# Sums of weights and of left factors on VectorE, and weighted values of two heads by turns, in a four-layer float32 transformer kernel on one core

## The chip, the core and the metric

One NeuronCore of a Trainium2 chip runs the whole program. The time is the device time of one execution in microseconds (us). The profiled execution is a single one, taken by the hardware profiler. Engines: TensorE (PE; its weight loads are PEld), VectorE (DVE), ScalarE (ACT), GpSimd (POOL), SyncE (SP, which issues most DMAs).

## What is computed

Two models run one after the other on 512 tokens of width 1024: two layers of the first block, then two layers of the second. Everything is float32. The parts that matter here, cut from the reference:

```python
# first block, per layer: one of two attentions has no positions (4 heads of 64)
z = einsum(q_blk, kt) * scale
log_stay = where(causal, log_sigmoid(-z), 0)
attn = where(causal, exp(log_sigmoid(z) + cumsum_of_later(log_stay)), 0)
o_b = einsum(attn, vt)                       # the weighted values
...
# second block, end of each layer: gated feed-forward, hidden width 2816
up = rmsnorm(x) @ w_gate_up
x = x + (silu(up[..., :2816]) * up[..., 2816:]) @ w_down
```

## The kernel before

Activations are kept transposed (features on the 128 partitions, 512 tokens along a tile) in `self.x`. A float32 product is made of three float32r products: each operand is split into a rounded part and a rest, by an ACT copy (`hi`, `xh`, ...) and a DVE subtraction (`lo`, `xl`, ...); `mm3` (L225 to L227) issues the three matmuls.

The whole program is written out in one order, and each engine executes its own instructions in that order. Weights come through a list of chunks made by `make_plan`. A chunk has raw tiles of 128x1024 (512 KB, loaded by SP, 6 buffers) and units, each a pair `hi`/`lo` made by `put` (L132 on ACT, L133 on DVE; 4 buffers each). `tick` and `product` call `pump`, which emits the units of the chunks to come, and then `step`, which advances every background generator by one piece.

**Feed-forward of the second block.** Hidden tiles 0 to 5 are plain products (`fa`, `fv`). Tiles 6 to 21 go in 16 pairs over both layers (8 a layer, in groups of 3, 2 and 3 and then 3, 3 and 2, with the down projection `fd` of a group behind it). A pair takes seven half-size products (a Strassen-like scheme) in place of eight. For that the weight blocks are added up (`schunks`: `pre` makes two sums before the pair's first unit, `post1` and `post5` one each behind the first and the fifth; `add`, L327, four sums of 128x1024 a pair), and the normalized activations, the left factors, are added up once a layer (`factors`, L1005 to L1013, a background generator that runs while the plain products go on; its `put` splits them at L992 to L996). `spair` runs a pair: seven `product` calls with the keys 11, 1, 2, 4, 12, 3 and 22, of 24 matmuls of 256 columns each (L1049), and between them

- L1083, L1087, L1092: ACT copies `s1`, `p5` and `d` out of PSUM;
- L1094, L1100: DVE forms the gate half by half from the bank `A`; product 3 adds into the same bank, so it waits for L1094;
- L1071: Silu on ACT; L1103: the first half times `s1`, on POOL; L1109: the second half out of PSUM, on DVE; L237 and L238: the split of the result.

Product 11 of the next pair is issued ahead of product 22 of a pair.

**Attention without positions.** `mixer_b` is a background generator beside the projections of the first block. It runs four heads a layer, one after another; heads 2 and 3 follow 0 and 1. For each it ends with the weights `at` (L840, exp on ACT; L844, mask on POOL) and, a step later, four products of float32 with 64 columns of values (L850) into the head's 64 partitions of `po`. In the profile each shows as two instructions. The other attention's three value tiles `va` are made at the start of `mixer1` (L664, ones set by POOL at L666).

For comparison: the attention of the second block's last layer issues its weighted values at L1774 for two heads by turns, with the same shapes as L850.

Of the kernel before, what the change touches and what calls it, by code (L numbers as in the profile page):

```python
# [4 lines left out]
F32 = mybir.dt.float32  # L5
F32R = mybir.dt.float32r
I32 = mybir.dt.int32
AF = mybir.ActivationFunctionType
ALU = mybir.AluOpType
AX = mybir.AxisListType  # L10
MUL, ADD, SUB, MAX = ALU.mult, ALU.add, ALU.subtract, ALU.max
P = 128
S = 512
# [304 lines left out]
def schunks(name, w, c1, c2):  # L318


    b = [block(w, r, 4, c, 256) for r, c in ((0, c1), (0, c2), (512, c2), (512, c1))]

    b11, b12, b22, b21 = b
    box = {}

    def add(c, to, x, y):
        c.nc.gpsimd.tensor_tensor(to, x, y, op=ADD)  # L327

    def pre(c, r):

        box["t"] = c.pf.tile([P, 1024], F32, tag="t0", bufs=1, name=c.nm("t0")).rearrange("p (k c) -> p k c", k=4)
        add(c, box["t"], r[0], r[1])
        add(c, r[1], r[1], r[2])

    def post1(c, r):

        add(c, r[0], r[0], r[1])

    def post5(c, r):

        add(c, r[0], r[0], r[1])

    def temp(c, hi, lo, raws):
        c.put(hi, lo, box.pop("t"))

    u = [dict(unit(4, 256, whole, (b11,), 0), pre=pre, praws=(b11, b12, b22), post=post1),
         unit(4, 256, temp, (b11,), 0),
         unit(4, 256, whole, (b11,), 0),
         unit(4, 256, whole, (b22,), 1),
         dict(unit(4, 256, whole, (b21, b11), 1, 1), post=post5, praws=(b21, b11)),  # L350
         unit(4, 256, whole, (b12,), 1),
         unit(4, 256, whole, (b21,), 1)]
    out = [chunk(name, [], [x]) for x in u]
    out[0]["raws"] = b
    return out
# [116 lines left out]
class Kern(Ctx):  # L472
# [188 lines left out]
    def mixer1(self, l):  # L661
        nc = self.nc

        va = [self.pv.tile([P, 4, 2, 3, 64], F32, tag="va", bufs=3, name=self.nm("va")) for _ in range(3)]  # L664
        for g in range(3):
            nc.gpsimd.memset(va[g][:, :, :, 1], 1.0)  # L666
        vb = self.pv.tile([P, 4, 256], F32, tag="vb", bufs=1, name=self.nm("vb"))
        qT, kT = {}, {}

# [50 lines left out]
        oB = []  # L720
# [9 lines left out]
            self.finish(g)  # L730
        gE = self.bg(self.mixer_a_exp(st))
        v_chunk("v1", va[1], True)
        v_chunk("v2", va[2], True)
        self.finish(gB)
        oA = [None] * 2
        gA = self.bg(self.mixer_a(va, st, oA))
        ga, gb = [], []
# [40 lines left out]
    def mixer_b(self, qT, kT, vb, oB):  # L778
        nc = self.nc
        seg = {0: (0, 0, 512), 1: (1, 0, 384), 3: (1, 384, 128), 2: (2, 0, 256)}  # L780
        nc.scalar.preload_act_table_set("natural_log_exp_and_others")
        for hp in range(2):
            po = None
            for hh in range(2):
                h = 2 * hp + hh
                rs = slice(64 * hh, 64 * hh + 64)
                q, k = qT[("b", hp)], kT[("b", hp)]
                z = [self.ps() for _ in range(3)]
# [37 lines left out]
                for kt in (0, 1, 3, 2):  # L826
# [8 lines left out]
                        continue  # L835
                    for v in (ach, acl):
                        nc.tensor.matmul(z[b][:, o + P:o + n], lhsT=self.nones_r, rhs=v[kt], start=False, stop=(v is acl), skip_group_check=True)
                at = [self.t("at") for _ in range(3)]
                for b in range(3):
                    nc.scalar.activation(at[b][:, 0:wid[b]], z[b][:, 0:wid[b]], AF.Exp)  # L840
                ag = {kt: at[b][:, o:o + n] for kt, (b, o, n) in seg.items()}
# [2 lines left out]
                    nc.gpsimd.affine_select(out=d, in_=d, pattern=[[1, P]], compare_op=ALU.is_gt, fill=0.0, base=0, channel_multiplier=-1)  # L844
                del z, sp, sg, acc, a1, a2, sph, spl, ach, acl
                yield
                if po is None:
                    po = self.ps()
                for kt in range(4):
                    nc.tensor.matmul(po[rs, kt * P:S], lhsT=vb[:, kt, h * 64:(h + 1) * 64], rhs=ag[kt], start=(kt == 0), stop=(kt == 3))  # L850
                if hh == 1:
                    oB.append(self.split(po, "oB"))

    def mixer_a_scores(self, g, qT, kT, st):
        nc = self.nc
# [123 lines left out]
    def factors(self):  # L979
# [2 lines left out]
        nc = self.nc  # L982
        A = self.A = {k: [] for k in ("11", "12", "22", "1", "2", "3", "4")}
        H = (slice(0, 256), slice(256, 512))
        tt = nc.gpsimd.tensor_tensor

        def put(src, keys, scale=None, tiles=None, at=0):
            n = src.shape[-1]
# [12 lines left out]
        for j in range(5):  # L1001
            cur = None
            if j < 4:
                xa, xb = self.t("xa"), self.t("xb")
                for t, k in ((xa, j), (xb, j + 4)):  # L1005
                    nc.scalar.activation(t, self.x[k], AF.Copy, scale=self.ngain(k))
                    tt(t, t, self.Rb, op=MUL)
                a11, a21, a12, a22 = xa[:, H[0]], xa[:, H[1]], xb[:, H[0]], xb[:, H[1]]
                s14, s23 = self.t("s14"), self.t("s23")
                tt(s14[:, H[0]], a22, a21, op=SUB)  # L1010
                tt(s23[:, H[0]], a11, s14[:, H[0]], op=ADD)
                tt(s23[:, H[1]], a21, a11, op=SUB)
                tt(s14[:, H[1]], s23[:, H[0]], a12, op=SUB)  # L1013
                cur = a11, xb, s14, s23
            if last:
                a11, xb, s14, s23 = last
                if j % 2:
                    two = self.ft("Ah"), self.ft("Al")
                put(a11, ("11",), tiles=two, at=256 * ((j - 1) % 2))
                put(s14, ("1", "4"))  # L1020
                put(s23, ("2", "3"), scale=-1.0)
                rest.append(xb)
            last = cur
            yield
# [28 lines left out]
    def ffn(self, l, after, conv):  # L1053
# [22 lines left out]
        def spair(f, ah, al):  # L1076
# [22 lines left out]
            for nt in range(2):  # L1099
                nc.vector.scalar_tensor_tensor(a[nt][:, H[1]], half(A, nt), -1.0, half(p5, nt), op0=MUL, op1=SUB)  # L1100
            g = [act_a(a[nt], f + nt, False) for nt in range(2)]
            for nt in range(2):
                nc.gpsimd.tensor_tensor(g[nt][:, H[0]], g[nt][:, H[0]], half(s1, nt), op=MUL)  # L1103
            yield
            self.product(A, "22", False)

            def out():
# [997 lines left out]
```

## Time and profile before

| | us |
|---|---|
| three runs | 2769.3, 2763.86, 2762.52 |
| median | 2763.86 |
| profiled execution | 2763.89 |
| its span, first to last instruction | 2761.8 |
| PE busy | 2704.5 |
| DVE busy | 1615.7 |
| ACT busy | 1108.2 |
| POOL busy | 554.0 |

The span is what the trace covers; the execution's own time is 2.1 us longer. PE is busy for nearly all of it, so that a change shows in the time where PE idles, runs at a lower clock, or has less to do. "Busy" of PE counts the time in which a matmul is under way.

### The profile page before, as it was taken

The numbers are of one execution on the slowest core, as the hardware profiler recorded it, in microseconds if no ns is written. First come the engines' busy times: TensorE is split into PE (matmuls) and PEld (weight loads), VectorE is DVE, ScalarE is ACT, GpSimd is POOL, SyncE is SP. The second block draws the span as 40 slices with busy tenths as digits, with TensorE's granted clock in tenths as the row PEclk, the third lists the DMA queues.
The fourth block names the chain that finished last, engine by engine and source line by source line (L and its number), as shares of the span: only waits on it lengthen the run. The fifth ranks groups of instructions, "written<-read, shape, count | busy, mean of one in ns | idle before, by whom it ended". The sixth has DMA issues, their size and how long they took to land.

```text
span 2761.8 us, 36222 instructions
## 1 busy us (share of the span) xinstructions
PE 2704.5 (98%) x14462; PEld 2303.4 (83%) x14462; DVE 1615.7 (58%) x2254; ACT 1108.2 (40%) x1672; POOL 554.0 (20%) x509
## 2 busy tenths in 40 slices
PE   8999999999999999999999999999999999999997
PEld 7788888888878888788878887898988888879897
DVE  5644654455455365554566667676756656667655
ACT  4353332333344334332343354343443536534334
POOL 2110210001111011110031105344411001334423
PEclk9999999999999999999999999999999999999999
DMA  5232323332323223322223332232232113223231
GB/s 189 62 93 76 92 92 93 105 99 88 114 67 82 72 92 107 103 95 93 92 92 111 96 103 81 93 122 92 89 90 86 54 47 107 85 84 114 78 107 54
DMA packets 236424, 254.77 MB, mean 92 GB/s; under 512 B 19904, under 2 KB 212672, under 8 KB 235616
## 3 DMA queue, kind: packets, MB, share of 16 engines
q1 hardware_dynamic: 233808, 245.70, 28.9%
q0 software_dynamic: 1440, 5.97, 0.6%
q8 instruction: 113, 1.85, 0.3%
q10 hardware_dynamic: 1008, 0.80, 0.1%
q14 instruction: 55, 0.45, 0.1%
HBM read 248.20 MB, written 2.10 MB: 91 GB/s over the span
## 4 chain that ended last, share of the span: by engine, by line
PE 87%; DVE 5%; ACT 3%; issue 3%; POOL 2%; DMA 0%; ACTq 0%; POOLq 0%; SPq 0%; DVEq 0%
PE ps L225 23%; PE ps L227 23%; PE ps L226 23%; PE ps L1049 11%; DVE lo L133 2%; PE ps L948 1%; ACT hi L132 1%; PE ps L850 1%; PE ps L1722 1%; PE ps L793 1%; PE ps L874 1%; DVE x L656 0%; PE ps L1448 0%; PE ps L963 0%; DVE xl L241 0%
## 5 line engine op out<-in xcount | busy, mean ns | idle before, releaser
L133 DVE TENSOR_TENSOR lo<-raw,hi 128x1024 fp32r<-128x1024 f32 (+2 forms) x515 | 655.0, 1300 | 272.3 <-ACT hi L132 269.7
L225 PE MATMUL ps<-xh,hi 128*128 128x512 f32 x1712 | 676.0, 395 | 11.5 <-ACT hi L132 11.5
L227 PE MATMUL ps<-xh,lo 128*128 128x512 f32 x1712 | 670.2, 391 | 6.5 <-DVE lo L133 6.4
L226 PE MATMUL ps<-xl,hi 128*128 128x512 f32 x1712 | 669.4, 391 | 0.0
L132 ACT ACTIVATE hi<-raw 128x1024 fp32r<-128x1024 f32 (+2 forms) x515 | 505.8, 1012 | 303.7 <-PE ps L226 232.5
L225 PEld LDWEIGHTS ps<-xh,hi 128*128 128x128 f32 x1712 | 323.3, 189 | 80.6 <-ACT hi L132 12.3
L227 PEld LDWEIGHTS ps<-xh,lo 128*128 128x128 f32 x1712 | 323.1, 189 | 77.6 <-DVE lo L133 9.7
L226 PEld LDWEIGHTS ps<-xl,hi 128*128 128x128 f32 x1712 | 323.4, 189 | 65.5 <-issue 0.2
L225 PE MATMUL ps<-acth,hi 128*128 128x512 f32 (+1 forms) x736 | 280.1, 381 | 1.0 <-ACT acth L237 1.0
L226 PE MATMUL ps<-actl,hi 128*128 128x512 f32 (+1 forms) x736 | 279.9, 380 | 0.6 <-DVE actl L238 0.6
L227 PE MATMUL ps<-acth,lo 128*128 128x512 f32 (+1 forms) x736 | 279.6, 380 | 0.0
L1049 PE MATMUL ps<-Ah,hi 128*128 128x256 f32 x896 | 255.0, 285 | 11.0 <-DVE a L1094 9.9
L1049 PE MATMUL ps<-Al,hi 128*128 128x256 f32 x896 | 254.2, 284 | 0.0
L1049 PE MATMUL ps<-Ah,lo 128*128 128x256 f32 x896 | 254.1, 284 | 0.0
L656 DVE TENSOR_TENSOR x<-ps,x 128x512 f32<-128x512 f32 x168 | 115.4, 687 | 176.0 <-PE ps L227 176.0
L1049 PEld LDWEIGHTS ps<-Ah,hi 128*128 128x128 f32 x896 | 172.4, 192 | 13.4 <-ACT hi L132 10.8
L537 POOL TENSOR_TENSOR sq<-sq,sq 128x512 f32<-128x512 f32 (+1 forms) x73 | 97.2, 1337 | 423.7 <-ACT sq L531 423.2
L1073 POOL TENSOR_TENSOR y<-y,Rb 128x512 f32<-128x512 f32 x44 | 57.0, 1295 | 590.5 <-ACT y L1068 590.5
L327 POOL TENSOR_TENSOR raw<-raw,raw 128x1024 f32<-128x1024 f32 x48 | 127.7, 2661 | 234.8 <-DVE lo L133 151.1
L1049 PEld LDWEIGHTS ps<-Al,hi 128*128 128x128 f32 x896 | 172.4, 192 | 0.4
L1049 PEld LDWEIGHTS ps<-Ah,lo 128*128 128x128 f32 x896 | 172.4, 192 | 0.0
L225 PEld LDWEIGHTS ps<-acth,hi 128*128 128x128 f32 x736 | 138.4, 188 | 27.5 <-ACT acth L237 1.4
(401 smaller groups left out, 4082.5 us busy)
## 6 DMA issues: line engine op xcount, KB each, us to landing
raw<-in_w_up SPq DMA_DIRECT2D x88, 512.0 KB, 3.7
raw<-in_ffn_w_gate_up SPq DMA_DIRECT2D x88, 512.0 KB, 3.6
raw<-in_w_in SPq DMA_DIRECT2D x78, 512.0 KB, 4.7
raw<-in_w_down SPq DMA_DIRECT2D x44, 512.0 KB, 4.1
raw<-in_ffn_w_down SPq DMA_DIRECT2D x44, 512.0 KB, 3.8
raw<-in_od_w_in SPq DMA_DIRECT2D x20, 512.0 KB, 3.9
raw<-in_w_o SPq DMA_DIRECT2D x16, 512.0 KB, 3.7
raw<-in_xattn_wkv SPq DMA_DIRECT2D x16, 512.0 KB, 4.5
```

The source lines that it names most:

```text
L132: self.nc.scalar.activation(hi, raw, AF.Copy)
L133: self.nc.vector.tensor_tensor(lo, raw, hi.bitcast(F32), op=SUB)
L225: mm(out, lhsT=wh, rhs=xh, start=first, stop=False)
L226: mm(out, lhsT=wh, rhs=xl, start=False, stop=False)
L227: mm(out, lhsT=wl, rhs=xh, start=False, stop=last)
L327: c.nc.gpsimd.tensor_tensor(to, x, y, op=ADD)
L537: (nc.vector if dve else nc.gpsimd).tensor_tensor(acc[to], acc[to], q, op=ADD)
L656: self.nc.vector.tensor_tensor(self.x[j], ps, self.x[j], op=ADD)
L793: nc.tensor.matmul(z[b][:, o:o + n], lhsT=k[rs, kt * P:(kt + 1) * P], rhs=q[rs, kt * P:S], start=(kt != 3), stop=False, skip_group_check=True)
L850: nc.tensor.matmul(po[rs, kt * P:S], lhsT=vb[:, kt, h * 64:(h + 1) * 64], rhs=ag[kt], start=(kt == 0), stop=(kt == 3))
L1049: mm(o, lhsT=w, rhs=x, start=(first and nt == 0 and j == 0 and i == 0), stop=(j == 3 and i == 2), skip_group_check=True)
L1073: nc.gpsimd.tensor_tensor(t, t, self.Rb, op=MUL)
```

## The change

Four sums of weights a pair (L327), the sums of the left factors (L1010 to L1013) and the product L1103 go from POOL to DVE. The left factors' two scalings (ACT at L1006, POOL at L1007) become one DVE instruction. `factors` gets one more `yield`, between the sums and their split; `spair` has its second `yield` ahead of the product at L1103, not behind it. In `mixer_b` the weights of the first head of a pair are kept in a `va` buffer until those of the second are there; then the eight products of both go by turns. The third `va` tile is made later for that, behind the end of `mixer_b`. Three parts of the diff that only rename are left out.

```diff
     def add(c, to, x, y):
-        c.nc.gpsimd.tensor_tensor(to, x, y, op=ADD)
+        c.nc.vector.tensor_tensor(to, x, y, op=ADD)
...
-        va = [self.pv.tile([P, 4, 2, 3, 64], F32, tag="va", bufs=3, name=self.nm("va")) for _ in range(3)]
-        for g in range(3):
-            nc.gpsimd.memset(va[g][:, :, :, 1], 1.0)
+        va = []
+
+        def new_va():
+            va.append(self.pv.tile([P, 4, 2, 3, 64], F32, tag="va", bufs=3, name=self.nm("va")))
+            nc.gpsimd.memset(va[-1][:, :, :, 1], 1.0)
+        for g in range(2):
+            new_va()
...
         v_chunk("v1", va[1], True)
+        self.finish(gB)
+        new_va()
         v_chunk("v2", va[2], True)
-        self.finish(gB)
...
-                at = [self.t("at") for _ in range(3)]
+                if hh == 0:
+
+                    room = self.pv.tile([P, 4, 2, 3, 64], F32, tag="va", bufs=3, name=self.nm("at")).rearrange("p t a b c -> p (t a b c)")
+                    at = [room[:, S * b:S * b + S] for b in range(3)]
+                else:
+                    at = [self.t("at") for _ in range(3)]
...
-                if po is None:
-                    po = self.ps()
+                if hh == 0:
+                    first = ag
+                    continue
+
+                po = self.ps()
                 for kt in range(4):
-                    nc.tensor.matmul(po[rs, kt * P:S], lhsT=vb[:, kt, h * 64:(h + 1) * 64], rhs=ag[kt], start=(kt == 0), stop=(kt == 3))
-                if hh == 1:
-                    oB.append(self.split(po, "oB"))
+                    for i, a in enumerate((first, ag)):
+                        c = (2 * hp + i) * 64
+                        nc.tensor.matmul(po[64 * i:64 * i + 64, kt * P:S], lhsT=vb[:, kt, c:c + 64], rhs=a[kt], start=(kt == 0), stop=(kt == 3))
+                oB.append(self.split(po, "oB"))
...
-        tt = nc.gpsimd.tensor_tensor
+        tt = nc.vector.tensor_tensor
...
                 for t, k in ((xa, j), (xb, j + 4)):
-                    nc.scalar.activation(t, self.x[k], AF.Copy, scale=self.ngain(k))
-                    tt(t, t, self.Rb, op=MUL)
+                    nc.vector.scalar_tensor_tensor(t, self.x[k], self.ngain(k), self.Rb, op0=MUL, op1=MUL)
...
                 cur = a11, xb, s14, s23
+                yield
...
             g = [act_a(a[nt], f + nt, False) for nt in range(2)]
+            yield
             for nt in range(2):
-                nc.gpsimd.tensor_tensor(g[nt][:, H[0]], g[nt][:, H[0]], half(s1, nt), op=MUL)
-            yield
+                nc.vector.tensor_tensor(g[nt][:, H[0]], g[nt][:, H[0]], half(s1, nt), op=MUL)
```

The order on DVE in the second pair of a group, from the first pair's L1109 (the gate's second half, out of PSUM) to the second pair's L1094. Before:

```order
L1109 TENSOR_TENSOR a_13775<-ps_13673,a_13775 128x256
L238 TENSOR_TENSOR actl_13971<-a_13774,acth_13970 128x512
L238 TENSOR_TENSOR actl_13975<-a_13775,acth_13974 128x512
L133 TENSOR_TENSOR lo_14005<-raw_13563,hi_14004 128x1024
L133 TENSOR_TENSOR lo_14040<-raw_13772,hi_14039 128x1024
L1094 SCALAR_TENSOR_TENSOR a_14013<-ps_13874,d_14044 128x256
```

The same place in the change (L1121 and L1106 there are L1109 and L1094 here, L1116 is the product L1103):

```order
L1116 TENSOR_TENSOR a_13759<-a_13759,s_13690 128x256
L133 TENSOR_TENSOR lo_13914<-raw_13688,hi_13913 128x1024
L133 TENSOR_TENSOR lo_13946<-raw_13721,hi_13945 128x1024
L327 TENSOR_TENSOR raw_13721<-raw_13721,raw_13501 128x1024
L1121 TENSOR_TENSOR a_13759<-ps_13657,a_13759 128x256
L238 TENSOR_TENSOR actl_13959<-a_13759,acth_13958 128x512
L133 TENSOR_TENSOR lo_13989<-raw_13543,hi_13988 128x1024
L327 TENSOR_TENSOR t_13992<-raw_13756,raw_13821 128x1024
L327 TENSOR_TENSOR raw_13821<-raw_13821,raw_13917 128x1024
L133 TENSOR_TENSOR lo_14024<-raw_13756,hi_14023 128x1024
L327 TENSOR_TENSOR raw_13756<-raw_13756,raw_13821 128x1024
L1106 SCALAR_TENSOR_TENSOR a_13997<-ps_13856,d_14028 128x256
```

One sum now stands ahead of the gate's second half, and three more ahead of L1094 of the pair behind it. Of two equal instructions in a row one is shown.

The order on ACT among the plain products, at one step of the left factors (`Ah` is the rounded part of a factor, `hi` of a weight). Before:

```order
L237 ACTIVATE acth_13079<-a_12993 128x512
L1006 ACTIVATE xa_13084<-x_70,prm 128x512
L1006 ACTIVATE xb_13085<-x_74,prm 128x512
L992 ACTIVATE Ah_13096<-xa_13041 128x256
L992 ACTIVATE Ah_13100<-s_13047 128x512
L995 ACTIVATE Ah_13104<-s_13048 128x512
L132 ACTIVATE hi_13133<-raw_12766 128x1024
```

And in the change:

```order
L1083 ACTIVATE a_13343<-a_13343 128x512
L1004 ACTIVATE Ah_13347<-xa_13214 128x256
L1004 ACTIVATE Ah_13351<-s_13218 128x512
L1007 ACTIVATE Ah_13355<-s_13219 128x512
L132 ACTIVATE hi_13384<-raw_13107 128x1024
```

The two scalings are gone from ACT, and the split of a step's sums comes one step later than the sums.

The order on PE where a pair of heads in the first layer ends, in the change; before, the first head's four products stood by themselves some 140 rows earlier:

```order
L863 MATMUL ps_990<-at_671,vb_210 64x512
L863 MATMUL ps_990<-at_929,vb_210 64x512
L863 MATMUL ps_990<-at_671,vb_210 64x384
L863 MATMUL ps_990<-at_930,vb_210 64x384
L863 MATMUL ps_990<-at_671,vb_210 64x256
```

Products of head 0 (`at_671`) and head 1 (`at_929`, `at_930`) now follow each other in turn, into the two halves of one PSUM bank.

## Rows read from the trace of the kernel before

**Rows 1.** The page, part 1: busy time, share of the span and instructions of each engine.

```profile
PE 2704.5 (98%) x14462; PEld 2303.4 (83%) x14462; DVE 1615.7 (58%) x2254; ACT 1108.2 (40%) x1672; POOL 554.0 (20%) x509
```

**Rows 2.** Waits of PE: us in total, times, longest.

```profile
PE ps L225 <- ACT hi L132: 13.4, 4, 7.3
PE ps L1049 <- DVE a L1094: 9.9, 5, 2.0
```

**Rows 3.** Windows: length, busy us (count) of PE, PEld, DVE, ACT, POOL, granted clock, DMA.

```profile
1700.00:1715.00 15.00, 15.00 (x68) 12.42 (x67) 11.46 (x11) 7.33 (x13) 14.69 (x12) 1.00 0.19 57
...
1720.00:1735.00 15.00, 9.69 (x34) 7.03 (x33) 11.91 (x13) 7.53 (x14) 12.00 (x11) 0.77 0.22 71
2420.00:2435.00 15.00, 10.42 (x36) 7.86 (x36) 12.07 (x13) 7.08 (x12) 12.88 (x11) 0.77 0.19 58
```

**Rows 4.** Windows of 10 us around the five waits for L1094; the sum is over five.

```profile
2520.00:2530.00 10.00, 8.02 (x55) 7.84 (x54) 8.59 (x9) 2.70 (x5) 3.54 (x4) 0.83 0.32 107
2615.00:2625.00 10.00, 8.02 (x67) 7.84 (x67) 10.00 (x9) 2.60 (x3) 4.82 (x2) 1.00 0.22 61
sum 50.00, PE 40.09 PEld 39.10 DVE 48.17 ACT 13.43 POOL 23.84; mean PE 8.02 PEld 7.82 DVE 9.63 ACT 2.69 POOL 4.77
```

**Rows 5.** Groups by line on PE, then PE's timeline: start, us, instruction.

```profile
L850 PE MATMUL ps<-at,vb 128*64 128x512 f32 (+3 forms) x64 | 18.9, 439 | 0.0
L1774 PE MATMUL ps<-PT,mv 128*64 128x512 f32 (+3 forms) x64 | 9.5, 439 | 0.0
...
2161.01 2.37 PE L1774 MATMUL ps<-PT,mv 128*64 128x512 f32 x16
```

**Rows 6.** Timeline of DVE in the first group's second pair.

```profile
1803.16 0.74 DVE L1100 SCALAR_TENSOR_TENSOR a<-ps,p 128x256 f32<-128x256 f32 x2
1805.74 3.70 DVE L133 TENSOR_TENSOR lo<-raw,hi 128x1024 fp32r<-128x1024 f32 x3 [1.84 <-ACT hi L132]
1810.52 4.82 DVE L238 TENSOR_TENSOR actl<-a,acth 128x512 fp32r<-128x512 f32 x2 [0.43 <-ACT acth L237]
1815.27 4.56 DVE L133 TENSOR_TENSOR lo<-raw,hi 128x1024 fp32r<-128x1024 f32 x2
1819.76 0.74 DVE L1094 SCALAR_TENSOR_TENSOR a<-ps,d 128x256 f32<-128x256 f32 x2
...
1825.09 0.74 DVE L1100 SCALAR_TENSOR_TENSOR a<-ps,p 128x256 f32<-128x256 f32 x2
```

**Rows 7.** Timeline of POOL in the same pair.

```profile
1811.94 2.85 POOL L327 TENSOR_TENSOR t<-raw,raw 128x1024 f32<-128x1024 f32 x1
1814.87 2.74 POOL L327 TENSOR_TENSOR raw<-raw,raw 128x1024 f32<-128x1024 f32 x1
```

**Rows 8.** DVE while POOL is idle (timeline), and its shortest instructions (by tile: min/median/max).

```profile
1835.42 2.35 DVE L133 TENSOR_TENSOR lo<-raw,hi 128x1024 fp32r<-128x1024 f32 x2
...
1931.08 1.29 DVE L238 TENSOR_TENSOR actl<-a,acth 128x512 fp32r<-128x512 f32 x2 [0.42 <-ACT acth L237]
...
L993 DVE TENSOR_TENSOR Al<-xa,Ah x8: 412/668/1344, 1703.8 to 2433.8; 128x256 fp32r<-128x256 f32 x8
...
L996 DVE SCALAR_TENSOR_TENSOR Al<-s,Ah x8: 678/1766/1800, 1707.1 to 2434.7; 128x512 fp32r<-128x512 f32 x8
```

**Rows 9.** The first stretch of left factors: timelines of PE, ACT and DVE.

```profile
1724.37 0.67 PE L225 MATMUL ps<-xh,hi 128*128 128x512 f32 x1 [2.67 <-ACT hi L132]
...
1723.28 1.99 ACT L132 ACTIVATE hi<-raw 128x1024 fp32r<-128x1024 f32 x2
...
1724.07 1.77 DVE L996 SCALAR_TENSOR_TENSOR Al<-s,Ah 128x512 fp32r<-128x512 f32 x1
1725.76 3.95 DVE L133 TENSOR_TENSOR lo<-raw,hi 128x1024 fp32r<-128x1024 f32 x2
```

**Rows 10.** Groups by line on POOL: busy us, mean ns, idle time before and what ended it.

```profile
L327 POOL TENSOR_TENSOR raw<-raw,raw 128x1024 f32<-128x1024 f32 x48 | 127.7, 2661 | 234.8 <-DVE lo L133 151.1 <-issue 68.2 <-DMA raw<-in_ffn_w_gate_up 14.3
L327 POOL TENSOR_TENSOR t<-raw,raw 128x1024 f32<-128x1024 f32 x16 | 47.2, 2952 | 19.3 <-DMA raw<-in_ffn_w_gate_up 19.3
```

More of the change, by code (lines that the diff above doesn't have):

```diff
@@ L782, in mixer_b @@
         for hp in range(2):
-            po = None
             for hh in range(2):
-                h = 2 * hp + hh
                 rs = slice(64 * hh, 64 * hh + 64)
```

## The prediction

> **What bounds the kernel now.** I read the page first: PE is busy for 2704.5 of 2761.8 us [rows 1], so there is no other engine to relieve as such. A gain can come from three things only: PE's own work, its 57 us of idling, and stretches at a lower granted clock. Then the waits of PE, to see whose they are. Two lines carry 23 us of the idling, and both lie in the second block's feed-forward: PE waits for the rounded weights of ACT (13.4 us, four times), and for L1094 of DVE (9.9 us, five times) [rows 2]. Third, windows around these waits, to see what they cost with the clock in it; fourth, the timelines of DVE, POOL and ACT there, to see what is late. What idles elsewhere (the starts of layers, the end) the change does not touch.
>
> *The stretches of the left factors.* A stretch of 15 us at full rate holds 68 matmuls of 512 columns, 0.221 us each; the two stretches where the left factors are made hold 34 and 36, and their granted clock is 0.77 on average: after PE has idled, a part of them runs at the lower of its two levels, 1.2 and not 2.4 GHz [rows 3]. So 66 matmuls are lost, 14.6 us, of which the two stretches' idling is 5.3 and 4.6 us; the rest is clock. What is late there is not PE's data as such. POOL is busy 14.69 of 15 us [rows 3], while a step of the factors comes with every 24 matmuls, 5.3 us. ACT waits in order for POOL's sums before it can round the next weights, at 1723.28, when PE has stood still for them since 1721.7; and DVE, beside POOL, takes 1.77 us for an instruction whose shortest is 0.68, and 3.95 us for two subtractions that take 2.35 when POOL is idle [rows 8, 9].
>
> *The pairs.* In each of the five places PE stands still for 2.0 us ahead of product 3: PE is busy 40.09 of 50 us, one place also has a clock of 0.83 and 55 matmuls where the next has 67, 12 of 0.12 us or 1.4 us more [rows 4]. That makes 11.3 us. DVE comes to L1094 late: beside POOL's sums of weights (2.85 and 2.74 us) two subtractions take 4.56 us and two splits 4.82 [rows 6, 7]; with POOL idle the same take 2.35 and 1.29 [rows 8].
>
> **The change, part by part.**
>
> *Weighted values by turns.* The same count and the same shapes stand twice in the trace: one head after another, 64 instructions keep PE busy 18.9 us; two heads by turns, 64 take 9.5, since 16 lie in 2.37 us [rows 5]. PE is saturated in the projections that this runs beside, so the 9.4 us come off the end: **-9.4**. From below it could be nothing, if the two heads did not overlap; L1774 has the same halves of a bank, and nothing else to tell it apart, so I take all. The first head's weights wait a few steps in a `va` buffer; nobody else wants that buffer before the last value tile, and behind the late memset on POOL stand only value copies of that tile, which come several steps later. Nothing.
>
> *Left factors on DVE.* Per step POOL loses two scalings and four sums, ACT loses two scalings. DVE gets two instructions of 128x512 at 0.68 and four of 128x256 at 0.41, the shortest of such rows [rows 8]: 3.0 us a step, 12 us a layer. The other end for these is what DVE takes beside POOL, 1.77 [rows 9], but POOL has then little left there (one product with the norm, for each hidden tile). With the split (0.41 and twice 0.68, 1.8 us), a chunk of 48 matmuls (10.6 us) asks of DVE: 3.0 + 1.8, two subtractions 2.35, and two to four instructions of about 0.68, some 9 to 10 us. That is tight but fits, and the extra `yield` puts sums and split into different steps. For the weights that PE now lacks at 1721.7: PE is done with the chunk before the last at 1711.1, two times 5.3 us earlier. DVE is then about 1 us behind with a step of sums; an evacuation 0.7, a piece of the rotation tables 0.6, the split 1.8 with some 0.8 of waiting for ACT, and the two subtractions 2.35 end at about 1718.4, 3.3 us ahead of PE. Carried on in the same way the next two chunks are ready some 1.6 and 2 us ahead. So I take back 13.6 of the 14.6 us and leave 1 us for a late one: **-13.6**. From below: one of the stretches stays as it is, -7.3.
>
> *Sums of weights and the product L1103 on DVE.* Four sums at 1.2 us (half of 2.35, the row with the same shape and inputs) and two products at 0.41 [rows 8] come into DVE's order, 5.6 us a pair, and POOL has nothing left to do there. The other end for a sum is POOL's own mean, 2.66 to 2.95 us [rows 10]. What decides is the way from L1100 of one pair to L1094 of the next, since PE cannot start product 3 before it. Before, it is 1820.50 - 1803.16 = 17.3 us [rows 6]. In the new order: L1100 0.74, the wait for ACT 1.84, three subtractions 3.70, two products 0.8, a sum 1.2, L1109 0.74, the wait 0.43, two splits 1.29, two subtractions 2.35, three sums 3.6, L1094 0.74: 17.4 us. So this way gets no shorter. But it starts earlier. PE's seven products take 1825.09 - 1803.16 - 2.0 = 19.95 us, 2.85 each; product 3 could start 17.1 us behind the end of the last product 3. Before, L1100 itself came nearly 2 us behind that end, because DVE had two more slowed subtractions ahead of it; now these take 1.2 each and L1100 waits only for PE. So PE's stand shrinks from 2.0 us to 0.3, or to 1 where ACT has its copies to make in between; I take 0.7. Five times 1.3, and the 1.4 of clock: **-7.9**. With sums at 2.66 us each place would stand 5.8 us longer, +29 in all; with no stand at all it would be -11.3.
>
> New waits: `pre` on DVE waits for raw weights. POOL's sums waited 33.6 us for DMAs in all [rows 10], but early, when POOL had nothing to do; DVE comes to `pre` only behind L238 or the first `x` of the down projection, some 8 us later, when they have landed. Behind it would stand L1094 or the sums into `x`. The second `yield` lets L1103 come behind a subtraction that has waited for ACT anyway. Nothing for either.
>
> A rule that speaks against all this: the Trainium skill (VectorE: DVE Perf Modes, "The DRAIN you can't avoid") says that behind every VectorE instruction the pipe drains for about its duration less 266 ns before the next starts; as an estimate from that, a sum of 1.2 us would hold DVE 2.2 us, and the sum of the terms would be some 20 us worse. The trace disagrees: two subtractions lie in 2.35 us and three in 3.70 [rows 6, 8], so there is no such gap.
>
> *Sum.* 9.4 + 13.6 + 7.9 = 30.9 us off the profiled 2763.9 us: **2733 us**. That execution is at the median of the three runs (2763.86), so nothing is to be shifted.
>
> **The rivals.**
>
> 1. *The left factors make DVE late in place of POOL.* For it: 9 to 10 of 10.6 us is little room, and the first layer also has the rotation tables on DVE there. Against: nothing of DVE's is then slowed by POOL. One stretch kept whole is 7.3 us: 2740.
> 2. *The pairs keep their stand.* For it: the way to L1094 is 17.4 us against 17.3, and 5.6 us more work is in DVE's order. Against: the late start goes. Then 7.9 is lost: 2741. With rival 1 as well: 2748.
> 3. *The two heads do not overlap*, the change not doing what it says there: 9.4 is lost, 2742. Only the place differs from L1774.
> 4. *A sum holds DVE twice as long as a subtraction.* Priced by the subtractions beside POOL, 2.28 us (half of 4.56 [rows 6]): 4 times 1.1 in five places, +22: 2755, no measurable change. By the page named above the price would be nearly that. The rows with POOL idle speak against it.
> 5. *Slower: DVE's long durations are its own, not POOL's doing.* Then POOL leaves and nothing gets shorter. Each of the five places gets four sums at 2.28 on top of its 2.0 us, +46; the factors' 12 us a layer become about 30 (a step of two at 1.77 and four at about 1), on an engine whose free quarter of 53 us is 12, so +18 a layer; with the turns' -9.4 it is 2763.9 + 73 = 2837. It decides by what a subtraction takes when POOL is idle: 1.18 us [rows 8] excludes it as far as that row goes; from 1.9 us on this change would lose.
>
> **How the numbers follow.** The forecast 0.60, by itself 2726 to 2739; rival 1 0.13, rival 2 0.10, both 0.04, rival 3 0.03, rival 4 with other mixes near no change 0.05, rival 5 or another loss 0.04. Better than 2724 needs more than all 35 us of the three stretches: 0.01. The range 2724 to 2745 takes in the forecast and rivals 1, 2 and 3, some 0.85. Faster by over 0.3% (8.3 us, about what a measurement of this kernel tells from no change), that is below 2755.6: 0.91; within: 0.05; slower: 0.04.
>
> **What would show it.** L850's successor busy some 9.5 us, with 16 instructions in 2.37. In the two stretches of left factors no wait of PE for the weights' rounded part over 1 us and a clock of 1.0. The subtractions among the pairs at about 1.2 us throughout, the sums on DVE at 1.2, and PE's waits for L1094 at 0.3 to 1 us each in the same five places. I am wrong where sums take over 2 us, where PE waits for a subtraction behind the factors' sums, or where DVE stands in `pre` for a DMA.

## The result and the profile after

The changed kernel takes 2742.49 us (median of four runs, 2741.61 to 2745.73), the kernel before 2766.58 in the same comparison (2762.52 to 2769.88): a ratio of 0.9916, 95% interval 0.9897 to 0.9934, 23 us faster by the ratio, as are the gains over the kernel before that follow. The forecast was 2733, 31 us faster. The time lies inside the range of 2724 to 2745, but only because that range took in rival 2 (2741): it is outside the 2726 to 2739 that the forecast had for itself, and one of the three terms did not come, as will be seen.

The page and PE's waits after the change (in the waits: us in total, times, longest; L1061, L1106, L1112, L1121 are L1049, L1094, L1100, L1109 of before):

```profile
PE 2694.9 (98%) x14462; PEld 2300.6 (84%) x14462; DVE 1631.3 (60%) x2398; ACT 1099.8 (40%) x1656; POOL 299.2 (11%) x365
```

```profile
PE ps L225 <- ACT hi L132: 9.4, 2, 7.4
PE ps L1061 <- DVE a L1106: 7.0, 4, 1.8
...
PE ps L227 <- DVE lo L133: 2.8, 5, 1.1
PE ps L225 <- ACT acth L237: 2.8, 2, 2.3
```

The last two of these were, before the change:

```profile
PE ps L227 <- DVE lo L133: 8.5, 7, 3.0
...
PE ps L225 <- ACT acth L237: 1.0, 2, 0.5
```

PE's busy time fell by 9.6 us [rows 1]: the weighted values. The wait for rounded weights lost 4.0 us and two of its four times [rows 2], and the wait for VectorE's subtractions lost 5.7 us and two of seven: the left factors. So most of PE's idling in those two stretches had ended with a subtraction on VectorE, not with a rounding. But PE still stands 1.76 us ahead of product 3 in four places, where it stood 1.98 in five; and the longest wait for `acth`, 2.31 us, is new.

Two windows of 15 us in the stretches of left factors, which now come some 7 and 13.6 us earlier (the windows beside them also hold 67 or 68 matmuls at 1.00):

```profile
1705.00:1720.00 15.00, 15.00 (x68) 12.43 (x67) 12.03 (x19) 7.36 (x13) 1.76 (x2) 1.00 0.21 72
...
2415.00:2430.00 15.00, 15.00 (x68) 12.43 (x67) 13.34 (x17) 6.56 (x10) 3.03 (x2) 1.00 0.27 90
```

68 matmuls at a granted clock of 1.00, where 34 and 36 ran at 0.77 [rows 3]. POOL is busy 1.76 and 3.03 of 15 us, in place of 12 or more.

The weighted values of the first pair of heads, PE's timeline:

```profile
107.67 2.37 PE L863 MATMUL ps<-at,vb 128*64 128x512 f32 x16
```

16 instructions lie in 2.37 us, as those of the second block did [rows 5]; all 64 keep PE busy 9.49 us.

**Where the 21.1 us of the span came from.** The same instruction of PE in both timelines, behind a wait that both have; the last column is what the stretch above the row gave:

| PE behind the wait for | before | after | earlier by | of this stretch |
|---|---|---|---|---|
| values' second layer, L571 at the start of the second block | 1440.48 | 1431.96 | 8.52 | -8.5 |
| L580 of the feed-forward's norm | 1687.86 | 1680.94 | 6.92 | +1.6 |
| product 3 in the second pair of the first group | 1820.64 | 1805.70 | 14.94 | -8.0 |
| L227 (`hah`) ahead of the next feed-forward | 2283.36 | 2269.78 | 13.58 | +1.4 |
| the same product 3 in the next layer | 2523.33 | 2502.29 | 21.04 | -7.5 |
| the last L580 | 2754.12 | 2732.98 | 21.14 | -0.1 |

The third and fifth rows are the left factors (with one shortened stand of 0.2 each), the fourth and sixth the other pairs: these gave nothing. The second row is no part of the change: behind a wait of 1.37 us that both kernels have, near 1495, the granted clock is 0.89 over 15 us with 51 matmuls, where the kernel before had 1.00 and 58.

**Why PE still stands.** VectorE in the second pair of the first group:

```profile
1786.56 0.76 DVE L1112 SCALAR_TENSOR_TENSOR a<-ps,p 128x256 f32<-128x256 f32 x2 [0.43 <-PE ps L1061]
1789.15 1.23 DVE L133 TENSOR_TENSOR lo<-raw,hi 128x1024 fp32r<-128x1024 f32 x1 [1.84 <-ACT hi L132]
...
1793.34 1.23 DVE L133 TENSOR_TENSOR lo<-raw,hi 128x1024 fp32r<-128x1024 f32 x1 [1.15 <-ACT hi L132]
1794.60 1.22 DVE L327 TENSOR_TENSOR raw<-raw,raw 128x1024 f32<-128x1024 f32 x1
...
1798.87 1.23 DVE L133 TENSOR_TENSOR lo<-raw,hi 128x1024 fp32r<-128x1024 f32 x1 [0.66 <-ACT hi L132]
1800.01 1.22 DVE L327 TENSOR_TENSOR t<-raw,raw 128x1024 f32<-128x1024 f32 x1
1801.27 1.22 DVE L327 TENSOR_TENSOR raw<-raw,raw 128x1024 f32<-128x1024 f32 x1
1802.41 1.22 DVE L133 TENSOR_TENSOR lo<-raw,hi 128x1024 fp32r<-128x1024 f32 x1
1803.66 1.23 DVE L327 TENSOR_TENSOR raw<-raw,raw 128x1024 f32<-128x1024 f32 x1
1804.80 0.75 DVE L1106 SCALAR_TENSOR_TENSOR a<-ps,d 128x256 f32<-128x256 f32 x2
```

Sums and subtractions take 1.2 us each. L1112 starts as soon as PE lets it (0.43): 3.1 us behind the start of the product 3 before it (1783.43), where it was 5.1 (1798.09), nearly 2 us earlier in PE's terms. From there to the end of L1106 it is 1805.55 - 1786.56 = 19.0 us: longer than before (17.3, [rows 6]), and the two nearly cancel. Two waits for ScalarE are new, 1.15 and 0.66 us; and three sums, 3.7 us, stand between the last wait and L1106. ScalarE there:

```profile
1792.25 1.06 ACT L132 ACTIVATE hi<-raw 128x1024 fp32r<-128x1024 f32 x1 [1.34 <-issue]
...
1801.10 0.59 ACT L1104 COPY d<-ps 128x512 f32<-128x512 f32 x1 [1.31 <-PE ps L1061]
```

Its copy `d`, all that L1106 needs of it, is done at 1801.69, three microseconds before L1106. And the rounding at 1792.25 comes no sooner than before against PE: 8.8 us behind the start of that product 3, where it was 9.0.

### The profile page after: what moved, and what is told of

Same layout as the page of the kernel before. It is cut to its first block, busy times and chain, and to the rows that moved or that the text cites. A ratio compares the mean times of both kernels' runs of the same rounds, so it can differ in the third digit from the quotient of the medians.

```text
span 2740.7 us, 36103 instructions
## 1 busy us (share of the span) xinstructions
PE 2694.9 (98%) x14462; PEld 2300.6 (84%) x14462; DVE 1631.3 (60%) x2398; ACT 1099.8 (40%) x1656; POOL 299.2 (11%) x365
## 4 chain that ended last, share of the span: by engine, by line
PE 91%; DVE 4%; ACT 3%; issue 2%; POOL 1%; DMA 0%; ACTq 0%; POOLq 0%; SPq 0%; DVEq 0%
PE ps L225 24%; PE ps L227 24%; PE ps L226 24%; PE ps L1061 11%; DVE lo L133 1%; PE ps L960 1%; ACT hi L132 1%; PE ps L1734 1%; PE ps L796 1%; PE ps L886 1%; PE ps L1460 0%; PE ps L975 0%; PE ps L571 0%; PE ps L580 0%; DVE xl L241 0%
## 5 line engine op out<-in xcount | busy, mean ns | idle before, releaser
L133 DVE TENSOR_TENSOR lo<-raw,hi 128x1024 fp32r<-128x1024 f32 (+2 forms) x515 | 608.3, 1207 | 269.9 <-ACT hi L132 267.9
L227 PE MATMUL ps<-xh,lo 128*128 128x512 f32 x1712 | 669.1, 391 | 0.8 <-DVE lo L133 0.7
L227 PEld LDWEIGHTS ps<-xh,lo 128*128 128x128 f32 x1712 | 322.5, 188 | 70.8 <-DVE lo L133 2.9
L227 PE MATMUL ps<-acth,lo 128*128 128x512 f32 (+1 forms) x736 | 280.2, 381 | 0.0
L1061 PE MATMUL ps<-Ah,hi 128*128 128x256 f32 x896 | 255.8, 286 | 8.0 <-DVE a L1106 7.0
L1061 PE MATMUL ps<-Al,hi 128*128 128x256 f32 x896 | 254.2, 284 | 0.0
L1061 PE MATMUL ps<-Ah,lo 128*128 128x256 f32 x896 | 254.0, 284 | 0.0
L1061 PEld LDWEIGHTS ps<-Ah,hi 128*128 128x128 f32 x896 | 172.4, 192 | 10.3 <-ACT hi L132 7.7
L1061 PEld LDWEIGHTS ps<-Al,hi 128*128 128x128 f32 x896 | 172.5, 193 | 0.4
L1061 PEld LDWEIGHTS ps<-Ah,lo 128*128 128x128 f32 x896 | 172.5, 193 | 0.0
L226 PEld LDWEIGHTS ps<-actl,hi 128*128 128x128 f32 x736 | 138.8, 189 | 27.3 <-DVE actl L238 1.3
L227 PEld LDWEIGHTS ps<-acth,lo 128*128 128x128 f32 x736 | 138.9, 189 | 26.3
```

Source lines behind the costliest of these rows:

```text
L133: self.nc.vector.tensor_tensor(lo, raw, hi.bitcast(F32), op=SUB)
L226: mm(out, lhsT=wh, rhs=xl, start=False, stop=False)
L227: mm(out, lhsT=wl, rhs=xh, start=False, stop=last)
L1061: mm(o, lhsT=w, rhs=x, start=(first and nt == 0 and j == 0 and i == 0), stop=(j == 3 and i == 2), skip_group_check=True)
```

## The experiments

My theory after the result: each part stands by itself; the left factors are settled; in the pairs VectorE's *order* sets the stand, not what a sum costs. The rival was that the stands come from elsewhere (ScalarE's copy, the weights' buffers) or that the parts disturb each other. The line numbers of runs with late sums are two higher.

**The three parts alone, and two sums moved.** `e1_turns`, `e2_factors` and `e3_pairs` are the kernel before with one part of the diff each (a line or two of each is shown):

```diff
 e1_turns: the hunks of mixer_b and of the va tiles
+                    for i, a in enumerate((first, ag)):
 e2_factors: the hunks of factors
+        tt = nc.vector.tensor_tensor
+                yield
 e3_pairs: the hunks of schunks and spair
+        c.nc.vector.tensor_tensor(to, x, y, op=ADD)
```

> Only the weighted values by turns, on the kernel before. Theory (the terms add up, each at its own place): PE's work on these products falls from 18.9 us by 9.4, everything later comes 8.5 to 9.5 us earlier, and the two stretches of left factors and the five places ahead of product 3 stay as they were: about 2754. Rival (the time comes back further on, in a later wait or at a lower clock): the first two layers end 8.5 to 9 us earlier, but the whole is faster by less than 5 us, and the trace shows where it was given back.

Ratio 0.9962 (0.9949 to 0.9976), 2756.17 us, 10.5 us faster. The two stretches and all five stands of 1.98 us are there as before.

> Only the left factors on VectorE with the extra yield, on the kernel before. Theory: both stretches of left factors lose their waits of PE and their low clock, 14 to 15.5 us in all; the sums of weights stay on POOL, and PE still stands 2.0 us ahead of product 3 in five places: about 2749. Rival (the factors make VectorE late in place of POOL, here or in the pairs): PE waits for a subtraction in one of the stretches, 7 us of gain or less, about 2757.

Ratio 0.9943 (0.9930 to 0.9955), 2751.22 us, 15.8 us faster; no wait of PE is left in the stretches.

> Only the sums of weights and the first half's product on VectorE, on the kernel before. Theory A (the order of VectorE sets the stand: what it gains by running without POOL it gives back in sums that stand ahead of the gate): subtractions of 1.2 us, PE still stands about 1.8 us ahead of product 3 in four or five places, and the time is within 2 us of before, about 2763. Theory B (the prediction's: each stand shrinks to 0.7 us or less): 8 us faster, about 2756; in that case the four stands of the changed kernel would come from the factors or the turns.

Ratio 0.9999 (0.9990 to 1.0007), 2766.53 us: no change. PE's waits are those of the changed kernel:

```profile
PE ps L1049 <- DVE a L1094: 7.0, 4, 1.8
```

The four stands of 1.75 us thus come from this part, and not from the others. So theory A: the pairs' part is worth nothing by itself. The three alone make 26.6 us, the change 23.2, with intervals of some 2 to 5 us to either side of each: nothing in these runs says that the parts disturb each other.

`e4_late_sums` is the changed kernel with two sums taken out of `pre` and `post1` and issued ahead of the split of the chunk's third unit (the call of `ahead` is not shown):

```diff
         add(c, box["t"], r[0], r[1])
-        add(c, r[1], r[1], r[2])
-    def post1(c, r):
+    def ahead2(c, r):
+        add(c, r[1], r[1], r[2])
         add(c, r[0], r[0], r[1])
...
-         unit(4, 256, whole, (b11,), 0),
+         dict(unit(4, 256, whole, (b11,), 0), ahead=ahead2, praws=(b11, b12, b22)),
```

> The changed kernel with two of the four sums of a pair (the second of the two ahead of the pair, and the one behind the first unit) moved behind L1112, ahead of the split of the unit that needs them, where VectorE idles 1.84 us for ScalarE. Theory A (2.45 us of sums ahead of the gate's first half are what PE still waits for): the gate comes 2.45 us earlier, more than the 1.76 us that PE stands; the four stands vanish (under 0.3 us), and 4 times 1.76 plus up to 1.6 of clock are gained: about 2734 to 2736. Rival (the gate waits for ScalarE's copy, or PE for buffers of the weights): the stands stay at 1 us or more, or move to a wait for a weight's rounded part, and the time stays at 2741 to 2743.

2734.81 us, ratio to the kernel before 0.9883 (0.9869 to 0.9896). The stands ahead of product 3 are gone from PE's waits, as theory A has it, and a small new one has come:

```profile
PE ps L1063 <- ACT p L1101: 4.1, 10, 0.4
```

On VectorE the gate (L1108 here) starts behind one sum and one subtraction, and product 3 no longer waits for it:

```profile
1800.97 1.22 DVE L329 TENSOR_TENSOR t<-raw,raw 128x1024 f32<-128x1024 f32 x1
1802.11 1.22 DVE L135 TENSOR_TENSOR lo<-raw,hi 128x1024 fp32r<-128x1024 f32 x1
1803.24 0.75 DVE L1108 SCALAR_TENSOR_TENSOR a<-ps,d 128x256 f32<-128x256 f32 x2
...
1807.82 0.76 DVE L1114 SCALAR_TENSOR_TENSOR a<-ps,p 128x256 f32<-128x256 f32 x2 [0.63 <-PE ps L1063]
```

The wait of 2.31 us for `acth` in the down projection fell to 0.52 as well, what it was before the change.

**What POOL's work does to VectorE, and what the yield does.**

```diff
 e5_pool_beside, in spair of the changed kernel behind product 11
+            sq = self.t("sq")
+            for _ in range(8):
+                nc.gpsimd.tensor_tensor(sq, self.Rb, self.Rb, op=ADD)
 e6_yield_alone, in factors of the kernel before
+                yield
 e7_no_yield, in factors of the changed kernel
-                yield
```

> The changed kernel with eight sums of 128x512 a pair added on POOL, behind product 11, from constant inputs into a tile that nobody reads: nothing waits for their result. It measures what POOL's work by itself does to VectorE. Theory A (VectorE's subtractions and sums were long because POOL was busy beside them): VectorE's 128x1024 instructions beside these run to 2 us and more where the changed kernel has 1.2, and the way to the gate gets longer by 4 us or more a pair; PE stands 4 us or more in the second pairs: 2765 to 2800. Rival (the durations were VectorE's own or those of the operations): 1.2 us throughout, stands of 1.8 us, about 2743.

Theory A: 2771.33 us, ratio to the kernel before 1.0019 (1.0009 to 1.0028), 29 us above the changed kernel for work that nobody waits for. PE stands 26.0 us in the pairs, up to 4.3 at a time, where it stood 7.0 in the changed kernel; the granted clock of the profiled execution is 0.990 and not 0.994. VectorE in the second pair of the first group, POOL's eight sums ending at 1805.1:

```profile
1798.10 0.74 DVE L1124 TENSOR_TENSOR a<-ps,a 128x256 f32<-128x256 f32 x2
1799.26 2.92 DVE L238 TENSOR_TENSOR actl<-a,acth 128x512 fp32r<-128x512 f32 x2 [0.43 <-ACT acth L237]
1802.11 2.06 DVE L133 TENSOR_TENSOR lo<-raw,hi 128x1024 fp32r<-128x1024 f32 x1
1804.09 2.06 DVE L327 TENSOR_TENSOR t<-raw,raw 128x1024 f32<-128x1024 f32 x1
1806.18 1.23 DVE L327 TENSOR_TENSOR raw<-raw,raw 128x1024 f32<-128x1024 f32 x1
1807.32 1.22 DVE L133 TENSOR_TENSOR lo<-raw,hi 128x1024 fp32r<-128x1024 f32 x1
```

While POOL works the two splits take 2.92 us for 1.29, a subtraction or a sum 2.06 for 1.22; from the moment that POOL is idle they are back. L1124, with one operand in PSUM, keeps its 0.74 throughout. The Trainium skill (SBUF — State Buffer, "Who interferes with whom") says that a VectorE instruction with two inputs in SBUF contends with a GpSimd instruction that reads SBUF, and that one with at most one SBUF input, outside the perf modes that use two ports, does not; the trace agrees, by 2.06 against 1.22 and by the unchanged 0.74.

> The kernel before with nothing but the extra yield between the sums of the left factors and their split; sums and scalings stay on POOL and ScalarE. POOL's work a step there is 7.7 us (two products with the norm at 1.5 and 1.67, four sums of 0.9 to 1.35), and a step then comes every 10.6 us and not every 5.3. Theory A (it was POOL's lateness in the order of ScalarE): POOL keeps up, the waits of PE in both stretches go, 12 us or more are gained: about 2752 to 2756. Theory B (it was VectorE, slowed by POOL beside it): PE still waits for a rounded part or a subtraction in each stretch, less than 7 us are gained: 2760 or more.

Theory A, and more of it than I had thought: 2751.80 us, ratio 0.9948 (0.9935 to 0.9960), 14.4 us faster. The yield alone does what `e2_factors` does, with all sums on POOL:

```profile
1715.00:1730.00 15.00, 15.00 (x68) 12.42 (x67) 12.46 (x14) 9.57 (x15) 11.66 (x11) 1.00 0.21 72
```

> The changed kernel without the extra yield: sums and scalings on VectorE, one step every 5.3 us. VectorE then has 3.1 us of sums and 1.8 of split in each of four steps, with 1.2 of subtractions a step and evacuations on top, some 7 us of 5.3, and falls behind by 6 to 8 us in four steps; four units lie ahead. Theory A (the yield is needed): PE waits 2 to 4 us for a rounded part or a subtraction in each stretch, about 2748 to 2752. Theory B (POOL's leaving is enough, the lead of the units covers it): within 1 us of the changed kernel, about 2742.5.

Theory A: 2749.23 us, ratio to the kernel before 0.9939 (0.9926 to 0.9951), some 6.7 us behind the changed kernel. PE waits 3.54 us for a subtraction in the first stretch and 1.17 in the second; in the first the clock falls as before:

```profile
1710.00:1725.00 15.00, 11.39 (x38) 8.56 (x37) 13.42 (x22) 7.42 (x13) 2.14 (x2) 0.77 0.20 72
```

VectorE is the late one there, busy 13.42 of 15 us, while POOL has 2.14.

**Which part of the pairs is needed.** `e8_copy_first` takes away the wait of 0.4 us that `e4_late_sums` had left (`settle` issues the second half and the split that the pair before has put off):

```diff
 e8_copy_first, in spair of e4_late_sums
-            self.settle()
             p5 = self.t("p5")
             nc.scalar.copy(p5, D)
+            self.settle()
 e9_order_on_pool, in schunks of e8_copy_first
-        c.nc.vector.tensor_tensor(to, x, y, op=ADD)
+        c.nc.gpsimd.tensor_tensor(to, x, y, op=ADD)
 e10_factors_pool, in factors of e8_copy_first
-        tt = nc.vector.tensor_tensor
+        tt = nc.gpsimd.tensor_tensor
-                    nc.vector.scalar_tensor_tensor(t, self.x[k], self.ngain(k), self.Rb, op0=MUL, op1=MUL)
+                    nc.scalar.activation(t, self.x[k], AF.Copy, scale=self.ngain(k))
+                    tt(t, t, self.Rb, op=MUL)
 e11_one_late_sum, in schunks of e4_late_sums: the sum ahead of the pair stays in pre
+        add(c, r[1], r[1], r[2])
     def ahead2(c, r):
-        add(c, r[1], r[1], r[2])
```

> The kernel with two late sums (e4_late_sums) and one more edit: in spair ScalarE's copy of product 1 (p5) stands ahead of the second half and the split of the pair before, not behind them. In e4_late_sums PE waits 0.4 us in ten pairs for that copy, which stands behind a split that waits for VectorE. Theory: the ten waits (4.1 us) go and nothing new comes, since ScalarE idles 3.5 us ahead of that split: about 2730.5 to 2731. Rival (the split comes later and PE waits for it, or the next buffer is late): 2733 or more.

2728.38 us, ratio 0.9865 (0.9850 to 0.9880): a little better than expected. Of PE's waits in the pairs one of 0.9 us is left, in the last pair of all:

```profile
PE ps L1063 <- DVE a L1114: 0.9, 1, 0.9
```

> The fastest kernel so far (e8_copy_first) with the four sums of weights a pair back on POOL, in e8's order. Theory A (with the order mended the sums still have to leave POOL): a sum takes 2.7 us there and VectorE's subtractions beside it 2.3 and more; the two late sums hold ScalarE's next rounding 3 us longer, and PE stands in the pairs again, 1 to 2 us in four or five places: 2735 to 2745. Theory B (the order was all): no stands, within 2 us of e8, 2727 to 2730.

Theory A, somewhat worse than I had it: 2747.14 us, ratio 0.9930 (0.9916 to 0.9945), 19 us behind `e8_copy_first`. PE's waits have the stands again:

```profile
PE ps L1063 <- DVE a L1108: 12.1, 5, 2.7
```

VectorE in the second pair of the first group shows why, two splits and two subtractions at the durations of before [rows 6]:

```profile
1796.90 4.90 DVE L240 TENSOR_TENSOR actl<-a,acth 128x512 fp32r<-128x512 f32 x2 [0.64 <-ACT acth L239]
1801.71 4.56 DVE L135 TENSOR_TENSOR lo<-raw,hi 128x1024 fp32r<-128x1024 f32 x2
```

> e8_copy_first with the left factors' sums and scalings back on POOL and ScalarE, the extra yield kept. Theory (from the run with the yield alone: it is the yield that freed these stretches, not the engine): within 1.5 us of e8, 2727 to 2730. Rival (VectorE is needed there): a wait of PE of 1 to 3 us in one of the two stretches, 2731 to 2736.

2726.96 us, ratio 0.9860 (0.9846 to 0.9874): not to be told from `e8_copy_first`. With the yield, POOL and VectorE do the left factors equally well, as far as these intervals tell. By its median this is the fastest kernel of the study, 15.5 us below the change.

> The changed kernel with only one of the four sums of a pair moved behind L1112 (the one behind the first unit), not two as in e4_late_sums. Theory (the stand is what VectorE has to do ahead of the gate, sum by sum): the gate comes 1.22 us earlier, each of the four stands falls from 1.76 to about 0.5 us, 4.9 us and up to 1.6 of clock gained: about 2736 to 2738. Rival (a stand goes only when all is moved, or it was the place and not the length): stands of 1.5 us or more, 2740 or more.

2732.68 us, ratio 0.9881 (0.9865 to 0.9897), below what I had expected. In PE's waits the stands fell as the theory has it, sum by sum:

```profile
PE ps L1063 <- DVE a L1108: 2.0, 4, 0.5
```

1.76 less 1.22 is 0.54; measured 0.49. The rest of the gain over the changed kernel is around it: the wait in the down projection is 0.80 and not 2.31, and the clock stays at 1.00 in the pairs, where the changed kernel lost some 1.6 us twice. Moving one sum does as much for the time as moving two in `e4_late_sums`, 0.9881 and 0.9883: the wait for ScalarE's copy `p`, 4.1 us, is not on this kernel's list.

## Why the prediction was right and wrong

**Weighted values by turns, -9.4.** Right: 18.94 us of PE's work became 9.49. What comes later is 8.5 us earlier by the trace, 10.5 (7 to 14) by the runs of `e1_turns`. Of the missing 0.9 us in the trace, 0.16 is a longer first wait for weights (7.26, then 7.42); the rest I cannot place.

**Left factors, -13.6.** The size is right: -15.1 in the trace, both stands of 0.2 taken off. The reason is not the one that I costed. The prediction counted 3.0 us of sums on VectorE against POOL's lateness, and named the extra `yield` in passing, as what "puts sums and split into different steps". The runs turn this round: the yield alone gives 14.4 us with POOL busy for 11.7 of 15 us; VectorE alone, without it, leaves the first stretch at 38 matmuls and 0.77. POOL needs 7.7 us for a step, VectorE with all that it has there 6.7 (in `e7_no_yield` one step's first instruction starts at 1704.68, the next one's at 1711.38, with no gap between); at one step every 5.3 us either is late, at one every 10.6 neither. VectorE alone is not nothing: without the yield the kernel is 6.7 us slower, so some 9 of the 15 us are there. What the yield does is two things: it halves the pace of the steps, and, since it stands between one step's sums and the split of the sums before, it puts three advances of the generator between sums and their split where there was one. The pace alone would explain the traces; no run separates the two. The sum came out because change and yield were made together; as far as the reason goes, that was luck. Rival 1, that VectorE becomes the late one, is what `e7_no_yield` shows; the yield keeps it out of the change.

**The pairs, -7.9.** Wrong: nothing came (by the table +1.4 and -0.1, with 0.2 twice for the two first stands). It is rival 2, priced at 2741, which had a chance of 0.10, and 0.04 with rival 1. The prices held: a sum 1.22 us, for 1.2; a subtraction 1.2 throughout. The step that failed is the sum of the way, 17.4 us, behind "So this way gets no shorter. But it starts earlier." It did start earlier, by 1.9 us, but the way was summed with the two waits that the trace of before showed, 1.84 and 0.43. Those for the other roundings were hidden there, since VectorE came late to them. Once it came early it waited 1.15 and 0.66 us for ScalarE, and 17.4 us became 19.0 against PE's 17.1. Starting 1.9 us earlier and taking 1.65 us longer than before leaves 0.3 us, and the stand fell by 0.2. The engine that was made faster here took over the waits that its lateness had covered; I had carried the old ones over. Why ScalarE's rounding comes no sooner is not shown. That PE holds it, by a buffer of the rounded weights that it must free first, fits that the rounding keeps its distance from PE's product 3 (8.8 and 9.0 us) and that PE ended a wait of ScalarE's for another rounding of the same pair before (1.30 us, at 1818.66); in the changed kernel the profile puts the wait of 1.34 us down to nothing, and another buffer was not tried.

*The fifth place*, the second pair of the first layer's group of two. Its stand went, but the load of down weights came later, the rounding of them waited 3.71 us for that load, and the second half of the gate stood behind it in VectorE's order: 2.31 us of PE in the down projection. The prediction had looked for VectorE standing in `pre` for a load; it was another load. SyncE's waits for POOL's sums before it can load, 72.3 us in all, have become waits for VectorE's sums and gate, 27.3 and 38.4 us.

**The other rivals.** Rival 3 (no overlap of heads) and rival 5 (VectorE's durations its own) are excluded, the first by 9.49 us, the second by `e5_pool_beside`, which makes the durations long and short at will. Rival 4, a sum that holds VectorE twice as long, is excluded too: the three instructions at 1800.01, 1801.27 and 1802.41 follow each other by 1.26 and 1.14 us. The rule of the Trainium skill named beside it (VectorE: DVE Perf Modes, "The DRAIN you can't avoid") would have them some 2 us apart, as an estimate. The same section adds that a next instruction that is not held starts earlier, which the prediction left out; the measured distances are in line with that.

**The sum.** In the trace: 8.5 + 8.0 + 7.5 gained, 1.6 lost to the clock near 1495 and 1.3 in the later pairs: 21.1 us of span, against 30.9 forecast. The pairs account for most of the difference.

## What to carry to other kernels

When work moves from a slow engine to a fast one, sum the fast engine's order again from the start of the waiting chain, with every wait that its earlier arrival uncovers, not with the waits of the old trace. What stands between the last input of a released instruction and that instruction is the first thing to move: two sums, shifted into a place where the engine idled anyway, made a part worth nothing into one worth 8 us, and with the copy moved 14. The new order does not replace the faster engine: with the sums back on POOL the same order was 19 us slower. And of two edits made together, such as another engine and a slower pace, run each alone: for the left factors the one-word edit gave by itself what both gave.

## What was not expected of the hardware

**The clock after a short stand falls or stays, and PE's busy time does not tell which.** `e3_pairs` has four stands of 1.75 us ahead of product 3. Windows of 15 us, each from 2 to 2.5 us ahead of the matmul behind the stand:

```profile
1820.00:1835.00 15.00, 13.25 (x99) 13.07 (x98) 10.06 (x14) 5.75 (x7) 0.00 (x0) 0.89 0.16 55
...
1984.00:1999.00 15.00, 13.25 (x98) 13.07 (x97) 10.02 (x15) 5.75 (x7) 0.00 (x0) 0.89 0.19 61
2527.00:2542.00 15.00, 13.25 (x111) 13.08 (x110) 11.55 (x16) 5.92 (x8) 0.00 (x0) 1.00 0.21 71
2622.00:2637.00 15.00, 13.25 (x98) 13.07 (x98) 10.06 (x14) 5.75 (x7) 0.00 (x0) 0.89 0.16 57
```

PE is busy 13.25 us in all four; three run 98 or 99 matmuls of 256 columns, one 111: 1.5 us. Before, one of five such stands had it, in the changed kernel one of four. Where it falls, eight matmuls or so of 512 columns follow each other by 0.43 us and not 0.23, at 1.2 and not 2.4 GHz; in the changed kernel behind the wait of 2.31 us:

```profile
1918.80 0.63 PE L225 MATMUL ps<-acth,hi 128*128 128x512 f32 x1
1919.23 0.63 PE L226 MATMUL ps<-actl,hi 128*128 128x512 f32 x1
1919.66 0.57 PE L227 MATMUL ps<-acth,lo 128*128 128x512 f32 x1
1920.07 0.39 PE L225 MATMUL ps<-acth,hi 128*128 128x512 f32 x1
1920.30 0.39 PE L226 MATMUL ps<-actl,hi 128*128 128x512 f32 x1
```

So a stand of 2 us cost 2 or 3.5 here, and the median can move by more than the idle time that one profile shows. The kernel before spreads over 7 us (2762.5 to 2769.9), `e10_factors_pool`, without these stands and without the waits among the left factors, over 1 (2726.9 to 2727.8). The spread goes more with the latter: `e2_factors`, with all five stands and none of those waits, spreads over 2 us, `e3_pairs`, with four stands and those waits, over 6. The clock moves with it: in the fifteen executions of the kernel before beside `e1_turns`, the two of under 2763 us have a granted clock of 0.994, the seven of over 2769 us one of 0.991 or 0.992. No run changes the clock alone, so that it makes the spread is likely and not shown.
